# Five engine programs in one critical section: without a block, opened by ScalarE, with semaphores cleared behind waits

## The chip, the cores and the metric

The kernel runs on one core of a Trainium2 chip. The metric is the device time of one execution in microseconds (us); the figure of a version is the median of its runs. The profile shows one execution; its span, from the first to the last recorded instruction, is somewhat shorter than the device time of that same execution.

## The reference

The kernel computes a low-rank (LoRA) update on top of its input. All of it is float32.

```python
batch, seq, d_model, r = 16, 512, 768, 16
# x: (16, 512, 768), A: (768, 16), B: (16, 768), scale = 0.5
def reference(x, A, B, scale):
    lora = np.matmul(np.matmul(x, A), B)
    return (x + scale * lora).astype(np.float32)
```

x has 8192 rows of 768 numbers, 25.2 MB; as much is written. A and B are 48 KB each.

## The kernel before

**Tiles and stages.** The rows are cut into six parts (`PARTS`, 64 tiles of 128 rows in all) that lie in three rooms of SBUF; the first room is used again by the last part. Eight tiles make a group, and there are eight groups. A group passes through five engines: ScalarE casts its first half to 16 bits and GpSimd its second half (`narrowed`, line 167); VectorE transposes both halves in blocks of 32 (`turned`, line 237); TensorE multiplies with A (`projected`, line 270); ScalarE scales the result into a block-diagonal operand (`spread`, line 201); TensorE multiplies with B (`raised`, line 288); VectorE adds the product to x in place (line 250). Ahead of the groups, A and B are loaded and rearranged once (lines 173 to 231, 299 and 206).

**Transfers.** SyncE issues every DMA, all into one queue: the loads of parts 0 and 1 (line 136), A (145), B (149), the loads of parts 2 to 4, and then stores (140) as the sums come, with the two loads of the last part in between as soon as the first room has been stored.

**Order and waits.** The order on every engine is written out by hand, and the engines meet only over semaphores that the kernel counts itself. The programs stand inside `tile_critical`, a section that the framework does not reorder. On entry one engine, SyncE if no other is named, executes a NOP that raises a semaphore (line 129), and all five engines wait for it in a branch (recorded under line 354). Inside the section `nc.Block` gives each engine a block of its own, entered and left by a jump; at the block's end all five engines drain and meet at a barrier (`programs.close()`, line 317). Then GpSimd clears the kernel's semaphores but one in a single range (line 320), waits until the last four stores have landed (line 321) and takes 64 off the remaining one, `s_out` (line 322). On leaving the section, the engine that opened it collects a signal of every engine (under line 129 too), and the framework ends with two barriers of all engines and a clear of its own semaphores (line 354).

Of the kernel before, what the change touches and what calls it, by code (L numbers as in the profile page):

```python
# [26 lines left out]
def kernel(  # L27
# [8 lines left out]
    nc = tc.nc  # L36
# [40 lines left out]
    sems = []  # L77
# [31 lines left out]
    s_ready, s_zero, s_bm = sem("s_ready"), sem("s_zero"), sem("s_bm")  # L109
    s_nact, s_npool = sem("s_nact"), sem("s_npool")  # L110
    s_turned, s_y, s_spread = sem("s_turned"), sem("s_y"), sem("s_spread")
    s_lora, s_sum = sem("s_lora"), sem("s_sum")

    s_free = [sem(f"s_free{p}") for p in range(PAIRS)]
    s_out0, s_out1, s_out = sem("s_out0"), sem("s_out1"), sem("s_out")

    MMS = 2 * NC
    THIRD = MMS // 3
# [7 lines left out]
    STORED = list(dict.fromkeys(groups_for(*st) for st in STORES))  # L126

    section = ExitStack()
    section.enter_context(tc.tile_critical(no_gpsimd_drain=True))  # L129
    programs = ExitStack()  # L130
    block = programs.enter_context(nc.Block(no_gpsimd_drain=True))

    @block.sync
    def _(e):
        def load(ld):
            e.dma_start(out=held(*ld), in_=memory(x2, *ld)).then_inc(s_load[ld], 16)  # L136

        def store(st, done):
            e.wait_ge(s_sum, STORED.index(groups_for(*st)) + 1)
            e.dma_start(out=memory(out2, *st), in_=held(*st)).then_inc(done, 16)  # L140

        load(LOADS[0])
        load(LOADS[1])
        e.wait_ge(s_ready, 1)
        e.dma_start(  # L145
            out=a_rows[0 : NC * APART : APART, :], in_=A.rearrange("(c e) r -> c (e r)", e=64)
        ).then_inc(s_a, 16)
        e.wait_ge(s_brows, 1)
        e.dma_start(out=b_rows[0 : R * APART : APART, :], in_=B).then_inc(s_b, 16)  # L149
        for ld in LOADS[2:5]:  # L150
            load(ld)
        for st, done in zip(STORES, (s_out0, s_out0, s_out1)):
            store(st, done)
        e.wait_ge(s_out0, 32)
        load(LOADS[5])
        e.wait_ge(s_out1, 16)
        load(LOADS[6])
        for st in STORES[3:]:
            store(st, s_out)
# [8 lines left out]
            out=xh[g % 2][:, ds(q * SUB, SUB), :], in_=held(*where[t], SUB)  # L168
        ).then_inc(done, 1)

    @block.gpsimd
    def _(e):
        e.memset(a_rows[0 : NC * APART], 0.0).then_inc(s_ready, 1)  # L173
        e.memset(b_rows, 0.0).then_inc(s_brows, 1)  # L174

        e.sem_inc(s_spread, 1)
        for s in s_free[2:]:
            e.sem_inc(s, 1)
        e.memset(pick, 0.0).then_inc(s_pick, 1)
        e.memset(w_bd.rearrange("p c k m -> p (c k m)").bitcast(fp32), 0.0)  # L180
        for t in y_bd:
            e.memset(t.rearrange("p s m -> p (s m)").bitcast(fp32), 0.0)  # L182
        e.wait_ge(s_pick, 1)
        e.affine_select(  # L184
            out=pick, in_=pick, compare_op=mybir.AluOpType.not_equal, fill=1.0, base=0,
            pattern=[[0, NQ], [-APART, Q]], channel_multiplier=1,
        ).then_inc(s_zero, 1)
        for g in range(NG):
            narrowed(e, e.tensor_copy, s_npool, g, 1)

    @block.scalar
    def _(e):
        e.wait_ge(s_zero, 1)
        e.wait_ge(s_b, 16)
        e.copy(out=b_half, in_=b_rows).then_inc(s_bh, 1)  # L195

        def spread(g):
            e.wait_ge(s_y, g + 1)
            for b in range(NQ):
                q = ds(b * Q, Q)  # L200
                last = e.mul(out=y_bd[g % 2][q, :, q], in_=y_ps[g % 2][q, :, :], mul=sc)  # L201
            last.then_inc(s_spread, 1)

        narrowed(e, e.copy, s_nact, 0, 0)
        e.wait_ge(s_bp, 1)
        e.copy(out=b_mm, in_=lora[0][:, 0, :]).then_inc(s_bm, 1)  # L206
        narrowed(e, e.copy, s_nact, 1, 0)
        for g in range(NG):
            spread(g)
            if g + 2 < NG:  # L210
                narrowed(e, e.copy, s_nact, g + 2, 0)

    @block.vector
    def _(e):
        e.wait_ge(s_a, 16)
        e.transpose(  # L216
            out=a_t[0 : NC * APART].rearrange("i k r c -> i (k r) c"),
            in_=a_rows[0 : NC * APART].rearrange("c (i k r) -> c (k r) i", k=2, r=R),
        ).then_inc(s_ready, 1)
        e.wait_ge(s_ready, 2)  # L220
        EACH = Q // APART
        for b in range(NC // EACH):
            last = e.tensor_copy(  # L223
                out=w_one[:, ds(b * EACH, EACH), :, :],
                in_=a_t[ds(b * Q, Q)].rearrange("i k r (c n) -> i c k r n", n=APART)[..., 0],
            )
        last.then_inc(s_ready, 1)
        e.wait_ge(s_ready, 3)
        e.wait_ge(s_zero, 1)
        for b in range(NQ):  # L230
            e.tensor_copy(out=w_bd[ds(b * Q, Q), :, :, ds(b * Q, R)], in_=w_one)  # L231

        def turned(g):
            for q, s in ((0, s_nact), (1, s_npool)):
                e.wait_ge(s, g + 1)
                v = xh[g % 2][:, ds(q * SUB, SUB), :].bitcast(fp32)
                last = e.transpose(out=v, in_=v)  # L237
            last.then_inc(s_turned, 1)

        turned(0)  # L240
        for p in range(PAIRS):
            e.wait_ge(s_lora, p + 1)
            e.sem_inc(s_free[p], 1)
        for g in range(NG):
            if g + 1 < NG:
                turned(g + 1)
            for p in range(PAIRS):
                xs = held(*where[g * GROUP + 2 * p], 2)
                e.wait_ge(s_lora, (g + 1) * PAIRS + p + 1)
                ins = e.tensor_tensor(  # L250
                    out=xs, in0=xs, in1=lora[p % 2], op=mybir.AluOpType.add
                )
                if g + 1 < NG or p + 2 < PAIRS:
                    ins.then_inc(s_free[p], 1)
                elif p + 1 == PAIRS:
                    ins.then_inc(s_sum, 1)
            if g + 1 in STORED[:-1]:
                e.drain().then_inc(s_sum, 1)  # L258

    @block.tensor  # L260
    def _(e):


        def projected(h, steps):
            if steps[0] == 0:
                e.wait_ge(s_turned, 1)
            xv = xh[h].rearrange("p s (c j k) -> p s c j k", c=NC, k=2)
            for m in steps:
                c, k = divmod(m, 2)
                last = e.matmul(  # L270
                    y_ps[h], w_bd[:, c, k, :], xv[:, :, c, :, k],
                    start=(m == 0), stop=(m == MMS - 1),
                )
            if steps[0] == 0:
                last.then_inc(s_turned, -1)
            elif steps[-1] == MMS - 1:
                last.then_inc(s_y, 1)

        def raised(h, p):
            if p == 0:  # L280
                e.wait_ge(s_spread, 1)
            free = s_free[(p + 2) % PAIRS]
            e.wait_ge(free, 1)
            t = lora[p % 2]
            mms = []
            for k in range(2):
                for n0, w in ((0, 512), (512, 256)) if k == 0 else ((0, 256), (256, 512)):
                    mms.append(e.matmul(  # L288
                        t[:, k, ds(n0, w)], y_bd[h][:, 2 * p + k, :], b_mm[:, ds(n0, w)],
                        start=True, stop=True,  # L290
                    ))
            if p == 0:
                mms[0].then_inc(s_spread, -1)
            mms[1].then_inc(free, -1)
            mms[-1].then_inc(s_lora, 1)

        e.wait_ge(s_bh, 1)
        for n0, w in ((0, 512), (512, 256)):
            last = e.matmul(  # L299
                lora[0][:, 0, ds(n0, w)], pick.rearrange("p b r -> p (b r)"),  # L300
                b_half[:, ds(n0, w)], start=True, stop=True,
            )
        last.then_inc(s_bp, 1)
        e.wait_ge(s_bm, 1)
        with e.Fori(0, NG // 2):
            for h in range(2):
                raised(1 - h, 0)
                raised(1 - h, 1)
                projected(h, range(0, THIRD))
                raised(1 - h, 2)  # L310
                projected(h, range(THIRD, 2 * THIRD))
                raised(1 - h, 3)
                projected(h, range(2 * THIRD, MMS))
        for p in range(PAIRS):
            raised(1, p)

    programs.close()  # L317
    nums = [s.num for s in sems]
    assert nums == list(range(nums[0], nums[0] + len(nums))) and sems[-1] is s_out
    nc.gpsimd.sem_clear(range(nums[0], nums[-1]))  # L320
    nc.gpsimd.wait_ge(s_out, 4 * 16)
    nc.gpsimd.sem_inc(s_out, -4 * 16)
    section.close()


# [33 lines left out]
```

## Time and profile before

| what | value |
|---|---|
| median of 3 runs | 124.8 us (124.76 to 125.47) |
| the profiled execution: its own time | 124.78 us |
| the profiled execution: its span | 122.8 us, 920 instructions |
| VectorE busy | 85.4 us (70%) |
| TensorE matmul busy | 58.1 us (47%) |
| ScalarE, GpSimd busy | 36.8 us, 26.4 us |
| DMA queue of the kernel | 2072 packets, 50.43 MB, 96.7% of 16 engines' span |
| HBM | 25.26 MB read, 25.17 MB written, 411 GB/s over the span |
| mean granted TensorE clock | 0.873 |

How to read it: busy time of an engine counts its datapath alone; branches, semaphore operations and the issuing of DMAs are recorded with a start and a duration but are not busy time. Some 2 us of the execution's time lie outside the span. Engine names with a q (SPq, POOLq) stand for the engine's instruction sequencer, DVE is VectorE, ACT ScalarE, POOL GpSimd, SP SyncE.

### The profile page before, as it was taken

Reading aid. Unit: us, or ns where it says so; the run is one execution under the profiler, and the core shown is the slowest. Engines: PE = TensorE matmul, PEld = TensorE weight load, DVE = VectorE, ACT = ScalarE, POOL = GpSimd, SP = SyncE. Lnnn points to the kernel's source line nnn. Section 1 sums busy time; section 2 is a strip of 40 time slices with the busy share of each in tenths; the row PEclk is TensorE's granted clock in tenths of the full one; section 3 lists DMA queues with packets and bytes.
Section 4 is the critical chain, followed back from the end, with each engine's and each line's share of the span. In section 5 each row is a group of like instructions: output and inputs, shape, how many; then the busy total and the mean of one; then the engine's idle time right before and its main releaser. Section 6 shows DMA issues by size and latency. Waiting matters only on the chain.

```text
span 122.8 us, 920 instructions
## 1 busy us (share of the span) xinstructions
PE 58.1 (47%) x338; PEld 33.5 (27%) x338; DVE 85.4 (70%) x56; ACT 36.8 (30%) x43; POOL 26.4 (22%) x19
## 2 busy tenths in 40 slices
PE   0000239948907944694584389449439645000000
PEld 0000015625503632362252145235224322000000
DVE  0004984089969999989999998999999859600000
ACT  0002958040199141707604080840400310000000
POOL 7703508000196001707100080440000000000000
PEclk9999999999995999769999958999995999655555
DMA  3999999799799895999999999899799799899990
GB/s 104 434 444 402 424 528 464 304 512 480 304 496 496 384 400 222 466 448 400 480 400 448 440 392 528 384 480 464 336 496 451 336 496 464 344 432 408 472 424 32
DMA packets 2073, 50.44 MB, mean 411 GB/s; under 512 B 252, under 2 KB 252, under 8 KB 536
## 3 DMA queue, kind: packets, MB, share of 16 engines
q1 hardware_dynamic: 2072, 50.43, 96.7%
q14 instruction: 1, 0.01, 0.0%
HBM read 25.26 MB, written 25.17 MB: 411 GB/s over the span
## 4 chain that ended last, share of the span: by engine, by line
DVE 40%; DMA 24%; PE 10%; DVEq 5%; ACT 2%; issue 2%; SPq 2%; POOL 1%; POOLq 0%
DMA x_sb<-in_x_dram 24%; DVE x_sb L250 23%; DVE xh L237 17%; PE lora_ps L288 6%; PE ps_yt L270 4%; DVEq L258 4%; ACT xh L167 2%; DVEq L317 1%; POOL a_rows L173 1%; SPq L145 1%; SPq L136 1%; SPq L149 0%; POOLq L354 0%; SPq L129 0%
## 5 line engine op out<-in xcount | busy, mean ns | idle before, releaser
L250 DVE TENSOR_TENSOR x_sb<-x_sb,lora_ps 128x1536 f32<-128x1536 f32 x32 | 54.0, 1738 | 2.6 <-PE lora_ps L288 2.6
L288 PE MATMUL lora_ps<-b_mm,y_bd 128*128 128x512 f16 (+1 forms) x144 | 33.0, 369 | 23.5 <-ACT y_bd L201 9.2
L167 POOL CAST xh<-x_sb 128x3072 f16<-128x3072 f32 x8 | 21.9, 2746 | 54.0 <-DMA x_sb<-in_x_dram 49.3
L270 PE MATMUL ps_yt<-xh,w_bd 128*128 128x256 f16 x192 | 28.9, 297 | 8.6 <-DVE xh L237 8.6
L237 DVE STREAM_TRANSPOSE xh<-xh 128x1536 f32<-128x1536 f32 x16 | 27.5, 1756 | 7.1 <-PE lora_ps L288 5.2
L167 ACT CAST xh<-x_sb 128x3072 f16<-128x3072 f32 x8 | 22.0, 2751 | 14.1 <-DMA x_sb<-in_x_dram 14.0
L270 PEld LDWEIGHTS ps_yt<-xh,w_bd 128*128 128x128 f16 x192 | 19.8, 106 | 18.0 <-DVE xh L237 10.9
L288 PEld LDWEIGHTS lora_ps<-b_mm,y_bd 128*128 128x128 f16 x144 | 13.5, 105 | 38.3 <-issue 24.1
L201 ACT ACTIVATE y_bd<-ps_yt 32x256 f16<-32x256 f32 x32 | 12.0, 374 | 36.1 <-PE ps_yt L270 35.8
L216 DVE STREAM_TRANSPOSE a_t<-a_rows 96x1024 f32<-96x1024 f32 x1 | 1.9, 1926 | 11.0 <-DMA a_rows<-in_A_dram 11.0
L299 PE MATMUL lora_ps<-b_half,pick 128*128 128x512 f16 (+1 forms) x2 | 0.8, 515 | 13.7 <-ACT b_half L195 13.7
L195 ACT ACT_TABLE_LOAD x1 | 1.3, 1283 | 11.6 <-DMA b_rows<-in_B_dram 11.6
L299 PEld LDWEIGHTS lora_ps<-b_half,pick 128*128 128x128 f16 x2 | 0.1, 112 | 13.7 <-ACT b_half L195 13.7
L223 DVE CAST w_one<-a_t 32x128 f16<-32x128 f32 x3 | 1.7, 573 | 0.1
L180 POOL MEMSET w_bd<- 128x1536 f32 x1 | 1.4, 1378 | 0.0
L173 POOL MEMSET a_rows<- 96x1024 f32 x1 | 0.9, 947 | 0.5 <-SPq L129 0.5
L231 DVE COPY w_bd<-w_one 32x384 f16<-32x384 f16 x4 | 1.0, 250 | 0.1
L182 POOL MEMSET y_bd<- 128x512 f32 x2 | 1.0, 521 | 0.0
L195 ACT CAST b_half<-b_rows 128x768 f16<-128x768 f32 x1 | 0.8, 831 | 0.0
L206 ACT CAST b_mm<-lora_ps 128x768 f16<-128x768 f32 x1 | 0.8, 798 | 0.0
L174 POOL MEMSET b_rows<- 128x768 f32 x1 | 0.7, 735 | 0.0
L184 POOL TENSOR_SCALAR_AFFINE_SELECT pick<-pick 128x128 f16<-128x128 f16 x1 | 0.3, 306 | 0.0
(5 smaller groups left out, 0.6 us busy)
## 6 DMA issues: line engine op xcount, KB each, us to landing
x_sb<-in_x_dram SPq DMA_DIRECT2D x2, 6144.0 KB, 36.5
out_dram<-x_sb SPq DMA_DIRECT2D x2, 6144.0 KB, 23.0
x_sb<-in_x_dram SPq DMA_DIRECT2D x3, 3072.0 KB, 15.1
out_dram<-x_sb SPq DMA_DIRECT2D x3, 3072.0 KB, 16.6
x_sb<-in_x_dram SPq DMA_DIRECT2D x1, 2304.0 KB, 9.9
out_dram<-x_sb SPq DMA_DIRECT2D x1, 2304.0 KB, 20.4
x_sb<-in_x_dram SPq DMA_DIRECT2D x1, 768.0 KB, 4.5
out_dram<-x_sb SPq DMA_DIRECT2D x1, 768.0 KB, 15.4
```

Source lines behind the costliest of these rows:

```text
L167: copy(out=xh[g % 2][:, ds(q * SUB, SUB), :], in_=held(*where[t], SUB)).then_inc(done, 1)
L173: e.memset(a_rows[0 : NC * APART], 0.0).then_inc(s_ready, 1)
L180: e.memset(w_bd.rearrange("p c k m -> p (c k m)").bitcast(fp32), 0.0)
L195: e.copy(out=b_half, in_=b_rows).then_inc(s_bh, 1)
L201: last = e.mul(out=y_bd[g % 2][q, :, q], in_=y_ps[g % 2][q, :, :], mul=sc)
L216: e.transpose(out=a_t[0 : NC * APART].rearrange("i k r c -> i (k r) c"), in_=a_rows[0 : NC * APART].rearrange("c (i k r) -> c (k r) i", k= ...
L223: last = e.tensor_copy(out=w_one[:, ds(b * EACH, EACH), :, :], in_=a_t[ds(b * Q, Q)].rearrange("i k r (c n) -> i c k r n", n=APART)[..., 0],)
L237: last = e.transpose(out=v, in_=v)
L250: ins = e.tensor_tensor(out=xs, in0=xs, in1=lora[p % 2], op=mybir.AluOpType.add)
L258: e.drain().then_inc(s_sum, 1)
L270: last = e.matmul(y_ps[h], w_bd[:, c, k, :], xv[:, :, c, :, k], start=(m == 0), stop=(m == MMS - 1),)
L288: mms.append(e.matmul(t[:, k, ds(n0, w)], y_bd[h][:, 2 * p + k, :], b_mm[:, ds(n0, w)], start=True, stop=True,))
```

## The change

The block is gone: the five programs become ordinary functions that are called one after the other inside the section, so that no engine jumps into or out of a block of its own and no barrier stands behind the programs. The section is opened (and its end collected) by ScalarE in place of SyncE. `s_sum` is allocated next to `s_out`, as the last but one. GpSimd now waits for the last of the six counts of `s_sum`, clears the 28 semaphores ahead of it, waits for the last stores, and clears `s_sum` and `s_out` with a second range clear in place of the subtraction.

```diff
-    s_lora, s_sum = sem("s_lora"), sem("s_sum")
+    s_lora = sem("s_lora")
 
     s_free = [sem(f"s_free{p}") for p in range(PAIRS)]
-    s_out0, s_out1, s_out = sem("s_out0"), sem("s_out1"), sem("s_out")
+    s_out0, s_out1 = sem("s_out0"), sem("s_out1")
+
+    s_sum, s_out = sem("s_sum"), sem("s_out")
...
     section = ExitStack()
-    section.enter_context(tc.tile_critical(no_gpsimd_drain=True))
-    programs = ExitStack()
-    block = programs.enter_context(nc.Block(no_gpsimd_drain=True))
-
-    @block.sync
-    def _(e):
+    section.enter_context(
+        tc.tile_critical(sync_engine=mybir.EngineType.Activation, no_gpsimd_drain=True)
+    )
+
+    def on_sync(e):
...
-    @block.gpsimd
-    def _(e):
+    def on_gpsimd(e):
...
-    @block.scalar
-    def _(e):
+    def on_scalar(e):
...
-    @block.vector
-    def _(e):
+    def on_vector(e):
...
-    @block.tensor
-    def _(e):
+    def on_tensor(e):
...
-    programs.close()
+    on_sync(nc.sync)
+    on_gpsimd(nc.gpsimd)
+    on_scalar(nc.scalar)
+    on_vector(nc.vector)
+    on_tensor(nc.tensor)
+
     nums = [s.num for s in sems]
-    assert nums == list(range(nums[0], nums[0] + len(nums))) and sems[-1] is s_out
-    nc.gpsimd.sem_clear(range(nums[0], nums[-1]))
+    assert nums == list(range(nums[0], nums[0] + len(nums))) and sems[-2:] == [s_sum, s_out]
+
+    nc.gpsimd.wait_ge(s_sum, len(STORED))
+    nc.gpsimd.sem_clear(range(nums[0], s_sum.num))
     nc.gpsimd.wait_ge(s_out, 4 * 16)
-    nc.gpsimd.sem_inc(s_out, -4 * 16)
+    nc.gpsimd.sem_clear(range(s_sum.num, s_out.num + 1))
     section.close()
```

## The prediction

> **What bounds the kernel now.** The page gives VectorE 70% and the DMA queue 96.7%, so I first asked for busy times by stretch, with the mean busy share of the 16 DMA engines and the bytes per second in the last two columns:
>
> ```profile
> core 0: us, PE busy (x) PEld busy (x) DVE busy (x) ACT busy (x) POOL busy (x), PEclk, DMA share, GB/s
> 0.00:1.90 1.90, 0.00 (x0) 0.00 (x0) 0.00 (x0) 0.00 (x0) 1.15 (x6) 1.00 0.00 0
> 1.90:3.00 1.10, 0.00 (x0) 0.00 (x0) 0.00 (x0) 0.00 (x0) 1.10 (x3) 1.00 0.89 274
> 3.00:20.00 17.00, 3.44 (x11) 1.30 (x12) 8.09 (x10) 6.87 (x5) 6.30 (x6) 1.00 1.07 448
> 20.00:60.00 40.00, 26.84 (x161) 16.19 (x159) 33.49 (x20) 18.18 (x21) 12.40 (x5) 0.91 0.98 413
> 60.00:100.00 40.00, 25.99 (x160) 15.38 (x160) 37.53 (x24) 11.75 (x19) 5.49 (x2) 0.91 1.01 434
> 100.00:120.00 20.00, 1.83 (x9) 0.62 (x8) 6.31 (x4) 0.00 (x0) 0.00 (x0) 0.63 0.99 428
> 121.60:122.80 1.20, 0.00 (x0) 0.00 (x0) 0.00 (x0) 0.00 (x0) 0.00 (x0) 0.50 0.00 0
> ```
>
> From 3 to 120 us all 16 DMA engines are occupied in every stretch (0.98 to 1.09; packets counted at a stretch's edge push a share over 1). Packet by packet, 16.0 are in flight in every microsecond of that time. The first packet of x starts at 1.98 us and the last ends at 121.57. So the span is three terms: 1.98 us until the first packet, 119.6 us of transfers at full occupancy, and 1.25 us after them. The compute engines and the block's end barrier at 107 us lie beneath the transfers. The change moves no byte, so it can act on the first and third term alone, and only by as much as SyncE's first issue moves, or the steps behind the last landing.
>
> Next the chain of waits, its first pieces (start, duration, what):
>
> ```profile
> 0.67 0.05 issue
> 0.72 0.02 SPq L129
> 0.74 0.02 issue
> 0.77 0.03 POOLq L354
> 0.80 0.15 issue
> 0.95 0.96 POOL a_rows L173
> ```
>
> SyncE's NOP at 0.72 opens the section, and GpSimd passes its branch at 0.77, 41 to 44 ns later. What matters more is SyncE itself, whose first transfers stand in the timeline of its sequencer:
>
> ```profile
> 0.97 0.86 SPq L136 DMA_DIRECT2D x_sb<-in_x_dram  x2
> ```
>
> Last, the steps under lines 354, 320 and 322 (count, shortest/median/longest ns, first and last start):
>
> ```profile
> L354 SPq DRAIN  x3: 7/7/7, 122.1 to 122.4; - x3
> L354 ACTq COMPARE_BRANCH  x1: 33/33/33, 0.8 to 0.8; - x1
> L354 SPq COMPARE_BRANCH  x1: 38/38/38, 0.8 to 0.8; - x1
> L354 PEldq COMPARE_BRANCH  x1: 174/174/174, 0.8 to 0.8; - x1
> L354 POOLq EVENT_SEMAPHORE_RANGE_CLEAR  x1: 67/67/67, 122.5 to 122.5; - x1
> L320 POOLq EVENT_SEMAPHORE_RANGE_CLEAR  x1: 200/200/200, 107.1 to 107.1; - x1
> L322 POOLq EVENT_SEMAPHORE  x1: 17/17/17, 121.9 to 121.9; - x1
> ```
>
> Each engine has exactly one branch at the start, the one that waits. SyncE has three drains at the end, the other engines two. A range clear of 29 semaphores took 200 ns, one of 6 took 67.
>
> **The start, part by part.** The trace's rows, to the nanosecond: the first barrier releases SyncE at 0.655 and ScalarE at 0.659. SyncE's NOP starts at 0.722. The other engines' branches start at 0.763 to 0.777 (TensorE 0.817), SyncE's own only at 0.804: an engine that waits for its own signal passes it 82 ns after giving it, one that waits for another's 41 ns after. The first issue starts at 0.966.
>
> *ScalarE opens.* Its NOP comes at 0.659 + 0.067 = 0.726 (the step from barrier to NOP that SyncE showed); SyncE passes at 0.726 + 0.041 = 0.767 in place of 0.804. That is **-0.037 us** on the path. ScalarE is delayed by about 40 ns instead, which is hidden: its next work waits for B until 11.50. Were SyncE's branch to take TensorE's 174 ns instead of 38, the start would lose 0.10; were the opening to cost nothing, with the issue one ordinary step (0.067) behind the barrier, it would gain 0.966 - 0.722 = 0.24. I take -0.04, which the rows of the other engines show directly.
>
> *No blocks behind jumps.* The plain jumps of the block have no row: between the barrier's end at 107.105 and SyncE's next step at 107.154 a block boundary was crossed in 49 ns, no more than between two steps inside a block (46 ns at 107.33). From SyncE's branch end (0.842) to the issue it is 124 ns, 64 over the 60 ns between the first two issues, and GpSimd shows a similar surplus. That surplus can belong to the waiting branch, which stays, or to a jump that the trace hides. So: 0 to -0.064; I take **0**, since all boundaries that are not waited at cost nothing. [...]
>
> Everything SyncE issues next (second load, A behind GpSimd's memset, B, three loads) follows into the same queue. The first two loads are 3.07 MB, 7 us of transfers at 440 GB/s, so a later issue of A or B by GpSimd's memset costs nothing at the end.
>
> *The block's end.* Drains and barrier from 106.7 to 107.1 vanish, as does the exit's collecting on SyncE at 107.2 to 107.4. The last store runs until 121.57: this is worth 0. If that cover were gone it would be worth 0.4. The added wait for `s_sum` on GpSimd has nothing behind it but the clear: GpSimd's last cast is over by 82 us, and the last sum comes at 106.31. Clearing 28 semaphores then takes some 0.2 us and ends 15 us before the last landing: 0.
>
> **The end, part by part.** Rows: the last of 64 landings counts at 121.910, GpSimd's wait and subtraction 121.934, its NOP 122.030, SyncE's NOP 122.069, SyncE's drains 122.121 and 122.185, the barrier gathered at 122.217, last row 122.796.
>
> *Clear in place of the subtraction.* From the two clears, 133 ns for 23 more semaphores is 5.8 each; two take 67 - 4 x 5.8 = 44 ns against 17, **+0.03**. If the wait can't ride on the clear and becomes a step of its own, another 0.08 (GpSimd's steps follow each other at 78 ns: 122.217 to 122.295). If the following step overlaps (28 ns between the clear at 122.470 and the drain behind it, against 79 behind the subtraction), 0.02 is won. So -0.02 to +0.11.
>
> *ScalarE collects the end.* SyncE's additional drain (64 ns) is now done early, if it is SyncE's whoever opens; ScalarE has only its barrier drain, some 69 ns behind its NOP as at 107.208 to 107.277. The barrier is gathered 122.069 + 0.013 + 0.069 + 0.032 = 122.18 in place of 122.217: **-0.03**, between 0 and -0.064.
>
> **Sum.** -0.04 + 0 + 0.03 - 0.03 = -0.04 us, against the profiled execution's own 124.78 (span 122.83 and 1.95 around it): 124.74. That execution stands 0.02 below the median of the runs, so the forecast is **124.7**. With all terms at their ends: -0.24 - 0.06 - 0.02 - 0.06 = -0.38, and +0.10 + 0.11 = +0.21.
>
> **The rivals.**
>
> *No effect at all.* The waiting branch keeps its 162 ns and what the opening gains is lost in the second clear. Time 124.8. For it: no jump rows; against it: the 41 ns by which SyncE waits for itself are plain.
>
> *The transfers end differently.* Twelve DMA engines finish by 120.66 and four between 121.10 and 121.56, each with packets of 0.91 us. An issue moved by 40 ns can deal the last packets otherwise: evenly, the end comes 0.9 earlier (123.9), with one more packet behind the slowest, 0.9 later (125.7). The three runs differ by 0.71 us already. Against it: nothing in the change alters sizes, order or queue.
>
> *Slower: the table load in front of the opening.* The program of ScalarE, which now opens the section, begins with a load of its activation table:
>
> ```profile
> L195 ACT ACT_TABLE_LOAD  x1: 1283/1283/1283, 11.6 to 11.6; - x1
> ```
>
> Now it stands behind the wait for B, where nobody minds it. With no block boundary between, it could come to stand ahead of ScalarE's NOP; then every engine, SyncE's first issue included, opens later by 1.28 us, and the time is 124.78 + 1.28 = 126.1. It decides from the moment the load precedes the NOP; placed between the NOP and the first cast it costs nothing. Against it: the load is recorded right ahead of the cast that needs it, and the NOP still lies outside the programs.
>
> *Faster by more than 1%.* Were there an instruction fetch behind each jump, removing jumps would take it away. The page counts one packet of the instruction queue in the span (8 KB, 0.31 us, at 93.2 us, while transfers run), none near the start. Even 0.31 and the best of every term give 124.1; passing 1% takes the lucky end of the transfers as well, 123.2. [...]
>
> **How the numbers follow.** A difference of about 1%, 1.25 us, is what a measurement of this kernel tells from no change. Chances: forecast 0.57, no effect 0.18, another end of the transfers 0.11, table load 0.07, the faster case 0.07. The first three lie within 1%: 0.86; slower 0.07, faster 0.07. The range reaches from the terms' ends, 124.4 to 125.0, a step toward the other ends of the transfers on both sides, since the runs before reach 125.47: 124.2 to 125.3.
>
> **What would show it.** After: NOP on ScalarE near 0.73, SyncE's branch near 0.77 and its first issue near 0.93; first packet near 1.95; 119.6 us of transfers; one drain fewer of SyncE behind the last landing; no rows of barrier at 107 us; a clear of some 44 ns at 121.9. Wrong would be: a first issue that moves by more than 0.25 us, transfers shorter or longer by over 1 us, or a step behind the last landing that took over 0.2.

## The result: the span got a little shorter, the time did not

Median after: **125.79 us** (14 runs, 124.67 to 126.33) against 124.72 us before (14 runs beside them, 124.40 to 125.47). The ratio of this set is 1.0067 with a 95% interval of 1.0046 to 1.0088 (the two medians alone stand 0.9% apart). That is less than the 1% that the prediction counts as no change, but the interval excludes no change, and the median lies above the predicted range of 124.2 to 125.3. The profiled execution after took 125.52 us.

The rows of instructions do not show the loss. The first view is the busy times by stretch of the kernel after (columns as in the prediction):

```profile
core 0: us, PE busy (x) PEld busy (x) DVE busy (x) ACT busy (x) POOL busy (x), PEclk, DMA share, GB/s
0.00:1.90 1.90, 0.00 (x0) 0.00 (x0) 0.00 (x0) 0.00 (x0) 1.14 (x6) 1.00 0.00 0
1.90:3.00 1.10, 0.00 (x0) 0.00 (x0) 0.00 (x0) 0.00 (x0) 1.10 (x4) 1.00 0.95 246
...
100.00:120.00 20.00, 2.31 (x13) 0.82 (x10) 6.75 (x4) 0.00 (x0) 0.00 (x0) 0.65 0.99 428
121.60:122.50 0.90, 0.00 (x0) 0.00 (x0) 0.00 (x0) 0.00 (x0) 0.00 (x0) 0.50 0.00 0
```

The transfers fill the span from 1.97 us to 121.18 us as they did before, and the span ends at 122.53 us, 0.30 us *earlier* than in the execution profiled before. The start is seen in the first pieces of the chain of waits (start, duration, what), then in SyncE's first issue in the timeline:

```profile
0.75 0.02 issue
0.78 0.03 POOLq L358
0.81 0.15 issue
0.96 0.96 POOL a_rows L173
```

```profile
0.93 0.85 SPq L137 DMA_DIRECT2D x_sb<-in_x_dram  x2
```

The steps under the lines of the section's exit (count, shortest/median/longest ns, first and last start), with the second clear on line 326:

```profile
L358 SPq DRAIN  x3: 7/7/7, 121.8 to 122.1; - x3
...
L358 SPq COMPARE_BRANCH  x1: 37/37/37, 0.8 to 0.8; - x1
```

```profile
L326 POOLq EVENT_SEMAPHORE_RANGE_CLEAR  x1: 45/45/45, 121.7 to 121.7; - x1
```

SyncE's first issue starts at 0.931 us instead of 0.966, and the new clear takes 45 ns: both as forecast.

Where the time went is seen by subtraction. Every run has its own time and its own span, and I call the difference the **time outside** (spans are given to 0.1 us). In 145 runs of the kernel before (those beside all the experiments below) it is 2.06 us in the mean and never above 2.51. In the 14 runs of the kernel after it is 2.98 us in the mean, while the mean span is 122.65 us against 122.78 before. In the profiled executions it is 125.52 - 122.53 = 3.0 us against 1.95.

The instruction rows end with the span, but packets of the DMA queues are recorded beyond it. First a stretch behind the span of the kernel after, then one of the kernel before (columns as above):

```profile
124.60:125.80 1.20, 0.00 (x0) 0.00 (x0) 0.00 (x0) 0.00 (x0) 0.00 (x0) 0.52 0.07 20
```

```profile
124.00:125.10 1.10, 0.00 (x0) 0.00 (x0) 0.00 (x0) 0.00 (x0) 0.00 (x0) 0.54 0.06 15
```

What moves there is instructions, by the kind that the profile gives their queue. In the kernel after a packet of 8 KB starts at 124.72 us and one of 16 KB at 124.83, which ends at 125.76; in the kernel before one of 16 KB runs from 124.03 to 125.02. The first memset starts 0.24 us into the span in both, and 125.76 - 0.24 = 125.52 and 125.02 - 0.24 = 124.78 are the times of the two executions. So in both the measured time ends with the 16 KB packet, which ends 3.23 us behind the span in place of 2.19.

The values after fall into two clusters. Over all 37 runs of the kernel after (the 14 above and two later sets) 19 lie between 1.8 and 2.43 us, like before, and 18 between 2.88 and 3.63 us, with nothing in between. I call a run **late** if its time outside is 2.8 us or more. Two runs in the table, one of e5 (126.63 us, and the 3.63 above) and one of e13 (127.09), are slow as a whole, over 1.5% above the fastest of their version, and are left out of the ratios alone: without them 17 of 36 runs of the kernel after are late, and e13's mean span is 122.76 us. So the question of the experiments is not what became slower in the span, but what makes some executions end about a microsecond later behind it.

### The profile page after: what moved, and what is told of

It is laid out like the page before. It is cut to its first block, busy times and chain, and to the rows that moved or that the text cites. A ratio compares the mean times of both kernels' runs of the same rounds, so it can differ in the third digit from the quotient of the medians.

```text
span 122.5 us, 908 instructions
## 1 busy us (share of the span) xinstructions
PE 56.9 (46%) x338; PEld 33.2 (27%) x338; DVE 85.7 (70%) x56; ACT 36.8 (30%) x43; POOL 26.5 (22%) x19
## 4 chain that ended last, share of the span: by engine, by line
DVE 40%; DMA 24%; PE 11%; DVEq 5%; ACT 2%; issue 2%; SPq 2%; POOL 1%; POOLq 0%; ACTq 0%
DMA x_sb<-in_x_dram 24%; DVE x_sb L248 23%; DVE xh L235 17%; PE lora_ps L285 6%; PE ps_yt L267 5%; DVEq L256 4%; ACT xh L168 2%; DVEq L131 1%; POOL a_rows L173 1%; SPq L146 1%; SPq L137 0%; SPq L150 0%; POOLq L358 0%; ACTq L131 0%
## 5 line engine op out<-in xcount | busy, mean ns | idle before, releaser
L285 PE MATMUL lora_ps<-b_mm,y_bd 128*128 128x512 f16 (+1 forms) x144 | 32.4, 364 | 25.2 <-ACT y_bd L200 10.6
L267 PE MATMUL ps_yt<-xh,w_bd 128*128 128x256 f16 x192 | 28.3, 293 | 8.4 <-DVE xh L235 8.4
L194 ACT ACT_TABLE_LOAD x1 | 1.3, 1283 | 11.6 <-DMA b_rows<-in_B_dram 11.6
```

The costliest lines, as they stand in the source:

```text
L267: last = e.matmul(y_ps[h], w_bd[:, c, k, :], xv[:, :, c, :, k], start=(m == 0), stop=(m == MMS - 1),)
L285: mms.append(e.matmul(t[:, k, ds(n0, w)], y_bd[h][:, 2 * p + k, :], b_mm[:, ds(n0, w)], start=True, stop=True,))
```

## Experiments

The theories in the order in which they came: (1) the opening by ScalarE does it; (2) the engines have to fetch their closing code from memory, and the changed instruction counts put that fetch at a bad moment; (3) the second range clear does it; (4) the block's end, which the prediction had priced at nothing, evens out the close. The profile records packets of a queue of the kind "instruction": in the kernel after one of 8 KB at 93.04 us of the span (and one of 40 bytes at its start), one of 8 KB at 124.72 and one of 16 KB at 124.83, both behind it. So theory 2 would leave marks that can be moved. Some expectations count as late what lies a little above 2.5 us; the counts here all use 2.8. At the head of a diff, "before" and "after" name the kernel that was edited.

| version | runs | median us | ratio to before (95%) | time outside, mean (range) | late | mean span |
|---|---|---|---|---|---|---|
| before, beside all of these | 145 | | | 2.06 (to 2.51) | 0 | 122.78 |
| after, first set | 14 | 125.79 | 1.0067 (1.0046 to 1.0088) | 2.98 (1.9 to 3.5) | 10 | 122.65 |
| e5, after, second set | 11 | 124.91 | 1.0017 (0.9991 to 1.0043) | 2.54 (1.9 to 3.6) | 4 | 122.65 |
| e18, after, third set | 12 | 125.22 | 1.0018 (0.9992 to 1.0045) | 2.46 (1.8 to 3.5) | 4 | 122.67 |
| e1, after, SyncE opens | 10 | 124.59 | 0.9995 (0.9969 to 1.0021) | 2.11 (1.8 to 3.2) | 1 | 122.64 |
| e2, before, ScalarE opens | 10 | 124.87 | 1.0008 (0.9989 to 1.0026) | 2.25 (1.8 to 2.5) | 0 | 122.68 |
| e3, after, 70 steps on ScalarE | 10 | 124.93 | 1.0017 (0.9990 to 1.0045) | 2.25 (1.8 to 3.4) | 1 | 122.75 |
| e4, after, 70 steps on SyncE | 4 | 125.74 | 1.0125 (1.0053 to 1.0198) | 2.32 (1.8 to 3.2) | 1 | 123.80 |
| e6, after, 8 steps on ScalarE | 11 | 124.83 | 1.0008 (0.9981 to 1.0036) | 2.17 (1.8 to 3.4) | 2 | 122.77 |
| e7, e1 and 5 steps on ScalarE | 11 | 124.83 | 1.0018 (0.9991 to 1.0046) | 2.36 (1.8 to 3.4) | 3 | 122.73 |
| e8, before, 2 steps on ScalarE | 11 | 124.65 | 0.9996 (0.9976 to 1.0015) | 1.98 (1.8 to 2.3) | 0 | 122.80 |
| e9, after, 3 steps on each engine | 12 | 124.90 | 1.0019 (0.9994 to 1.0045) | 2.41 (1.9 to 3.3) | 3 | 122.55 |
| e10, after, 9 steps on each engine | 7 | 125.50 | 1.0060 (1.0035 to 1.0084) | 2.34 (1.8 to 3.0) | 2 | 123.27 |
| e11, after, subtractions at the end | 12 | 125.21 | 1.0039 (1.0011 to 1.0067) | 2.62 (1.8 to 3.5) | 6 | 122.61 |
| e12, after, in the block | 12 | 124.55 | 0.9982 (0.9967 to 0.9997) | 1.93 (1.8 to 2.1) | 0 | 122.63 |
| e17, e12 again | 12 | 124.77 | 0.9993 (0.9974 to 1.0012) | 2.08 (1.7 to 2.4) | 0 | 122.66 |
| e13, after, barrier behind the programs | 12 | 125.21 | 1.0029 (1.0011 to 1.0047) | 2.43 (2.1 to 3.0) | 1 | 122.91 |
| e14, after, barrier ahead of the programs | 12 | 125.32 | 1.0050 (1.0022 to 1.0078) | 2.55 (2.0 to 3.4) | 5 | 122.98 |
| e15, after, ScalarE and TensorE held | 12 | 125.00 | 1.0019 (0.9999 to 1.0040) | 2.35 (2.0 to 2.9) | 1 | 122.69 |
| e16, after, the block's closing steps | 12 | 124.93 | 0.9999 (0.9982 to 1.0016) | 2.12 (1.8 to 2.5) | 0 | 122.80 |

e1 to e4 shared one chip and one set of runs of the kernel before, and so did e5 to e8, e9 to e12, e13 to e15, and e16 to e18.

### Which part: the opening or the block (e1, e2)

e1 takes the opening by ScalarE out of the change; e2 does that part alone.

```diff
 after
-    section.enter_context(
-        tc.tile_critical(sync_engine=mybir.EngineType.Activation, no_gpsimd_drain=True)
-    )
+    section.enter_context(tc.tile_critical(no_gpsimd_drain=True))
```

> The changed kernel with SyncE opening the section as before, the rest of the change kept. Theory A (the microsecond lies behind the span, because an engine's program with another number of instructions has its closing code at another place, where a further 8 KB of instructions has to be fetched behind the last instruction): ScalarE's program gets 2 recorded instructions shorter than in the changed kernel and SyncE's 3 longer, so if one of these two is the engine, the time outside the span falls from 3.0 to 2.0 us and the time to 124.7; if it is GpSimd, VectorE or TensorE it stays at 3 us and 125.7. Rival B (an engine other than SyncE that opens and collects the section makes the program's end slower): 2.0 us outside and 124.7 in any case. Rival C (the second clear is at fault): stays at 125.7. First issue of SyncE again at 0.966 us in all.

```diff
 before
-    section.enter_context(tc.tile_critical(no_gpsimd_drain=True))
+    section.enter_context(
+        tc.tile_critical(sync_engine=mybir.EngineType.Activation, no_gpsimd_drain=True)
+    )
```

> The kernel before with ScalarE opening the section and nothing else changed (blocks, barrier and subtraction kept). Rival B: 125.7, with some 3 us outside the span. Rival C: 124.7. Theory A: ScalarE's program gets longer and SyncE's shorter by a few instructions; 124.7 if the place that matters is not passed, 125.7 if it is, with the extra 8 KB packet behind the span. First issue of SyncE near 0.93 us in all.

Neither moves the median by a measurable amount. But e2 has no late run in 10, and e1, in which SyncE opens again, still has one at 3.23 us. So the opening isn't needed for a late run. It may not be without effect: five of e2's ten runs have 2.43 to 2.53 us outside, more than any of the 25 runs of the kernel before beside them (1.90 to 2.40).

### Moving the instruction fetch (e3, e4)

```diff
 after
+    s_pad = sem("s_pad")
     s_sum, s_out = sem("s_sum"), sem("s_out")
...
     def on_scalar(e):
+        for _ in range(70):
+            e.sem_inc(s_pad, 1)
         e.wait_ge(s_zero, 1)
```

> The changed kernel with 70 semaphore increments at the head of ScalarE's program, where it waits for B until 11.5 us anyway, so they cost nothing in the span (5.5 us at 78 ns each, over by 6.5 us). Theory A with ScalarE as the engine: its code passes the place long before the end, the fetch moves under the transfers, the time outside the span falls to 2.0 us and the time to 124.7. Theory A with another engine, and B and C: stays near 125.7.

In e4 the same 70 steps stand on SyncE, behind its first loads:

```diff
 after
             load(ld)
+        for _ in range(70):
+            e.sem_inc(s_pad, 1)
         for st, done in zip(STORES, (s_out0, s_out0, s_out1)):
```

> The changed kernel with 70 semaphore increments in SyncE's program behind the first loads, where it waits for the first sum from 5 to 35 us, so they cost nothing in the span. Theory A with SyncE as the engine: time outside the span falls to 2.0 us and the time to 124.7. Theory A with another engine, and B and C: stays near 125.7.

In e3 the fetch moved as meant: a packet of 8 KB that lay 2.2 us behind the span's end in the kernel after lies at 9.8 us in e3. One run of 10 is late all the same. e4 brought something else: its span is 1.1 us longer. Its queues, in the view of the DMA:

```profile
q1 hardware_dynamic: 2072, 50.43, 96.0%
q14 instruction: 3, 0.02, 0.0%
```

and the end of its transfers, from the busy times by stretch:

```profile
121.00:122.00 1.00, 0.00 (x0) 0.00 (x0) 0.00 (x0) 0.00 (x0) 0.00 (x0) 0.50 0.06 25
122.00:122.90 0.90, 0.00 (x0) 0.00 (x0) 0.00 (x0) 0.00 (x0) 0.00 (x0) 0.50 0.00 0
```

A further packet of 8 KB now starts at 13.0 us, amid the loads. From 121 to 122 us a share of 0.06 is left, one engine of 16: that one works until 122.43 us, the next-last until 121.54. In the kernel after, the last ends at 121.18. That the packet at 13.0 us holds up this engine is argued from the order of events; no run tested it. The packet itself took 0.32 us, which does not cover 1.1, and the packet at 9.8 us in e3, amid the loads too, had no such effect.

The large instruction packets within these spans are of 8 KB; those of 16 KB lie behind them, in the kernel after at 124.83 us. In e4 something that came with the 70 steps was not hidden beneath the transfers: its mean span is 123.80 us against 122.65.

### The change again, and instruction counts (e5 to e10)

e5 is the kernel after, unaltered.

> The changed kernel itself once more, on the chip of its neighbours here. Theory A (ScalarE's program, through its number of instructions, has its closing code at a place where a fetch of 8 KB is waited for behind the span) expects 125.7 us again, about 3 us outside the span in two of three executions. If it comes out at 124.8, the microsecond hung on the chip and not on the program.

e6 is e3 with 8 steps instead of 70:

```diff
 after
     def on_scalar(e):
+        for _ in range(8):
+            e.sem_inc(s_pad, 1)
```

> The changed kernel with 8 semaphore increments at the head of ScalarE's program, hidden under its wait for B. Theory A: 8 instructions move the place at which the fetch falls due 8 instructions closer to the kernel's end; the time outside the span changes from 3.0 us to between 2.0 and 2.6, the time to 124.8 to 125.2. Rival D (what counts is that ScalarE opens and collects while the blocks are gone, the number of instructions is immaterial): 125.7 and 3 us outside.

e7 adds 5 steps to e1, so that ScalarE executes 58 instructions, as in the kernel after (e1 has 53, three fewer than its expectation reckoned); e8 adds 2 to the kernel before, for the same number.

```diff
 e1
     def on_scalar(e):
+        for _ in range(5):
+            e.sem_inc(s_pad, 1)
```

> The changed kernel with SyncE opening the section, and with 5 semaphore increments in ScalarE's program, so that ScalarE's program has the same number of instructions (58 recorded) as in the changed kernel. Theory A with the number on ScalarE alone deciding: 125.7 us, 3 us outside the span. Rival D, or theory A with SyncE's number deciding: 124.6 as with SyncE opening alone.

```diff
 before
     @block.scalar
     def _(e):
+        for _ in range(2):
+            e.sem_inc(s_pad, 1)
```

> The kernel before with 2 semaphore increments in ScalarE's program, which make it 58 recorded instructions, as many as in the changed kernel; everything else is the kernel before. Theory A with ScalarE's executed instructions deciding: 125.7 us, 3 us outside. If the block's borders take room in the program without being executed, the place isn't met and it stays at 124.8, as rival D expects as well.

e9 and e10 pad all five engines at once. With 3 (GpSimd 2), each executes as many instructions as with the block; 9 go well past that.

```diff
 after
+        for _ in range(3):
+            e.sem_inc(s_pad, 1)
```

(on SyncE behind the first loads, on ScalarE and VectorE at the head of their programs, on TensorE ahead of its wait for `s_bh`; on GpSimd 2 behind its second memset)

> The changed kernel with as many executed instructions on each engine as the kernel with blocks that ScalarE opens: 3 semaphore increments more on SyncE, ScalarE, VectorE and TensorE, 2 on GpSimd, all in idle time. Theory E (the time outside the span scatters up to 3.6 us in some executions because the closing code of SyncE, GpSimd, VectorE or TensorE lies at another place in the instruction stream; executed instructions count): back to 1.8 to 2.5 us outside in every execution, median 124.8. Rival F (the barrier at the block's end, not the number of instructions, keeps the closing together): executions of 2.9 us and more outside stay, two or more of them in ten. Rival C (the second clear): they stay as well.

```diff
 after
+        for _ in range(9):
+            e.sem_inc(s_pad, 1)
```

(in the same places; on GpSimd 8)

> The changed kernel with 9 semaphore increments more on each engine (8 on GpSimd), which match the kernel with blocks if the borders of a block take room in the stream without showing as executed instructions. Theory E with that count: 1.8 to 2.5 us outside in every execution, median 124.8. Rivals F and C: executions of 2.9 us and more outside stay.

The second set of the change has a ratio of 1.0017 where the first had 1.0067, with 4 late runs in 11 where there were 10 in 14. The effect is a share of executions, and that share differs between sets, so the median of one set is a poor measure of it.

For theory 2 in the form that a program's number of instructions decides, these runs are bad. e8 has ScalarE's count of the kernel after and no late run in 11; e7 has the same count and 3 in 11; e9, with the block's counts on every engine and no block, has 3 in 12. The 8 KB packet did follow ScalarE's count where it is recorded (2.2 us behind the span's end at 58 instructions, 0.3 us at 66), but moving it left late runs in e6 and e3. As the cause, the place of this packet is out. That it adds to their number isn't excluded: e3, e6 and e1 together have 4 late in 31, less than the 18 in 37 of the change. The 16 KB packet is another matter: none of these edits was made to move it, and the part on what is open comes back to it.

e10's longer span has a place in its trace: in the closing, ScalarE's first drain starts 361 ns behind its NOP, in the kernel after 57 ns. Why isn't shown.

### The second clear, and the block with everything else (e11, e12)

```diff
 after
-    nc.gpsimd.sem_clear(range(s_sum.num, s_out.num + 1))
+    nc.gpsimd.sem_inc(s_sum, -len(STORED))
+    nc.gpsimd.sem_inc(s_out, -4 * 16)
```

> The changed kernel with two subtractions, of s_sum and s_out, in place of the second clear. Rival C: 1.8 to 2.4 us outside in every execution, 124.7. Theory E and rival F: executions of 2.9 us and more outside stay, some four in ten, median 124.9 to 125.7.

```diff
 after
+    programs = ExitStack()
+    block = programs.enter_context(nc.Block(no_gpsimd_drain=True))
 
-    def on_sync(e):
+    @block.sync
+    def _(e):
...
-    on_sync(nc.sync)
...
+    programs.close()
```

> The changed kernel with the block kept: ScalarE opens, the clears stand behind their waits, only the programs stand in blocks of their own with the barrier behind them. Theory E and rival F: no execution over 2.6 us outside, median 124.8. Rival C: executions of 2.9 us and more, median 125 or more.

This pair divides the change in two. Without the second clear 6 of 12 are late; with it and ScalarE's opening, but inside the block, none of 12, and all twelve lie between 1.8 and 2.1 us. Theory 3 is out, and what is missing in the kernel after is something of the block.

### What of the block: three partial substitutes (e13 to e15)

```diff
 after
     on_tensor(nc.tensor)
+    nc.all_engine_barrier()
```

> The changed kernel with one barrier of all engines behind the five programs and ahead of GpSimd's clears, without a block. Rival F (the barrier at the block's end keeps the closing together): 1.8 to 2.5 us outside the span in every execution, median 124.6 as with the block kept. Rival G (not the barrier, but the places of code that the block's borders make): executions of 2.8 us and more outside stay, a third of them or more, median 124.9 to 125.7.

```diff
 after
+    nc.all_engine_barrier()
     on_sync(nc.sync)
```

> The changed kernel with the same barrier of all engines ahead of the five programs. It delays SyncE's first issue by about 0.4 us, so the span is 123.0. If only the late barrier matters (F): executions of 2.8 us and more outside stay. If the number of instructions or of barriers matters and not their place in time: 1.8 to 2.5 us outside in every execution, as then behind the programs too. Rival G: they stay.

```diff
 after
+    s_late = nc.alloc_semaphore("s_late")
...
                 e.drain().then_inc(s_sum, 1)
+        e.drain().then_inc(s_late, 2)
...
     on_scalar(nc.scalar)
+    nc.scalar.wait_ge(s_late, 1)
+    nc.scalar.sem_inc(s_late, -1)
     on_vector(nc.vector)
     on_tensor(nc.tensor)
+    nc.tensor.wait_ge(s_late, 1)
+    nc.tensor.sem_inc(s_late, -1)
```

> The changed kernel with ScalarE and TensorE held behind their programs until VectorE has made the last sum (one wait each, no barrier), so that no engine is at the section's end ahead of 106 us, as with the block, but without a meeting of all. If it is the early arrival of these two (ScalarE at 97.6, TensorE at 104) that spreads the closing: 1.8 to 2.5 us outside in every execution, 124.6. If it takes the meeting of all engines (F), or code places (G): executions of 2.8 us and more stay.

The reason for e15 is in the steps under line 131 of the kernel after, the section's own collecting of its engines:

```profile
L131 ACTq EVENT_SEMAPHORE  x3: 17/38/38, 97.6 to 107.4; - x3
...
L131 ACTq DRAIN  x1: 1477/1477/1477, 97.7 to 97.7; - x1
L131 PEldq DRAIN  x1: 870/870/870, 103.5 to 103.5; - x1
L131 DVEq DRAIN  x1: 2442/2442/2442, 104.4 to 104.4; - x1
```

Without the block's end, ScalarE is through its program at 97.6 us and TensorE at 104.4; with it, both stay until all have met at 107.1. A barrier ahead of the programs (e14) leaves 5 late in 12 and adds 0.3 us to the first packet (2.31 us against 1.97). Holding engines at the end is another matter: e13 and e15 have 1 late in 12 each, 2 in 24 against 18 in 37. Their other runs aren't quite as before either, with means of 2.38 and 2.30 us against 2.06. Nor is there a gap at 2.8 us in these two: their late runs have 2.98 and 2.91 us, the next 2.66 and 2.58. So holding the engines at the end goes with fewer late runs, not with none, and e13's median of 125.21 us is not the 124.6 that was expected of a barrier that does it all.

### The block's closing steps without the block (e16 to e18)

The deciding set, on one chip: e16 is the kernel after with the drains and the barrier that the block would have executed, written out behind the plain functions; e17 is e12 again, e18 the kernel after again.

```diff
 after
     on_tensor(nc.tensor)
+    for e in (nc.scalar, nc.tensor, nc.vector, nc.sync):
+        e.drain()
+    nc.all_engine_barrier(sem_only=True)
```

> The changed kernel with the very instructions that the block puts behind the programs (a drain of four engines, the barrier of five by semaphores alone), but without a block, so that every engine executes the same instructions in the same order as in the next kernel, which keeps the block. If the end of the block does it (its drains and barrier together with the place that they give to the closing code): 1.8 to 2.4 us outside the span in every execution, and the same time as the next kernel, 124.6. If it is the block's borders alone, marks that are not executed (G): executions of 2.6 us and more stay, a third or more, median 125.0 or more.

> The changed kernel with the block kept, once more: ScalarE opens, both clears stand behind waits, programs in blocks. All theories that blame the block's removal: no execution over 2.5 us outside, 124.55 to 124.7, and no slower than the kernel before. If the earlier run of it owed its 0.9982 to its chip: 124.8 and some executions over 2.5.

> The changed kernel itself a third time, beside the two others on one chip. All theories: 2.8 us and more outside the span in a third to two thirds of the executions, median 124.9 to 125.8, span 122.65. Were it as even as the block's version here, the difference would hang on the chip.

There are four drains because the block drains four engines, not all five: GpSimd's rows under line 317 of the kernel before are semaphore steps alone. In e16 the four have their rows under the line of the loop, and run while the transfers do:

```profile
L320 ACTq DRAIN  x1: 1556/1556/1556, 95.4 to 95.4; - x1
L320 PEldq DRAIN  x1: 870/870/870, 101.4 to 101.4; - x1
L320 DVEq DRAIN  x1: 2440/2440/2440, 102.3 to 102.3; - x1
L320 SPq DRAIN  x1: 131/131/131, 105.1 to 105.1; - x1
```

e16 has 0 late in 12, with 2.12 us outside; e17 0 in 12, with 2.08; e18 4 in 12, with 2.46. With 0 in 24 against 4 in 12 this one set could still be luck (of all ways to place four late runs among these 36, 1 in 120 puts all four on e18), but it does not stand alone. Every version that executes the block's closing steps (e2, e8, e12, e16, e17 and the kernel before) has none: 0 in 57 beside 0 in 145. Every version that lacks them has some. And since e16 has no blocks and no jumps into or out of them, the closing steps suffice without the blocks. That last step rests on twelve runs: 0 in 12 for e16 alone beside 4 in 12 would come by chance once in 21 times. The medians of e16 and e17 both lie above the 124.6 that was expected. A fetch behind each jump, which the faster rival of the prediction supposed, shows no price here: e17 with its jumps has a median of 124.77 us, e16 without them 124.93.

e16 differs from e13 in little: GpSimd is not drained in e16, and the other four engines signal the barrier in a step of their own behind the drain. Which of these takes away the rest of the late runs isn't separated, and 0 in 12 against 1 in 12 is no difference by itself.

**A version that beats both?** The block kept, with ScalarE's opening and the clears (e12, e17), gives ratios of 0.9982 (0.9967 to 0.9997) and 0.9993 (0.9974 to 1.0012): a gain of 0.2% and of 0.1%, and the second interval includes no change. It has none of the late runs of the kernel after, and is hardly different from the one before.

## Why the prediction was right and wrong

**Right: what bounds the span.** Only the first and the third term of the span were to change. The transfers lasted from 1.967 to 121.179 us, 119.2 us against 119.6, with the same packets. The mean spans differ by -0.13 us (122.65 against 122.78).

**Right: ScalarE opens.** SyncE's branch starts at 0.769 us (forecast 0.767, before 0.804) and the first issue at 0.931: -0.035 us against -0.037. The first packet came 0.016 us earlier in this execution (1.967 against 1.983).

**Right: no blocks behind jumps, 0.** From the end of SyncE's branch to the first issue it is 125 ns, 124 before. The surplus that could have been a hidden jump is still there without the jumps, so it isn't theirs.

**Slightly off: clear in place of subtraction.** The clear took 45 ns, 44 forecast. But the next step follows 89 ns behind its start, where it followed 96 ns behind the subtraction: -0.007 us instead of +0.03. The step's duration was right; it had simply been hidden in the interval to the next one.

**Right sum, wrong detail: ScalarE collects the end.** From GpSimd's NOP to the gathered barrier it is 163 ns against 187, so -0.024 us (forecast -0.03). SyncE still shows three drains behind the last landing, not one fewer: its first simply begins earlier. (The prediction's "the other engines two" holds for three of them; GpSimd had three drains at the end as well.) From the last landing to the last row it is 0.89 us against 0.92.

**Right to give it little: the table load in front of the opening.** The load is still recorded at 11.6 us, ahead of its cast, so that rival's 126.1 did not come about. The rival of transfers that end differently named 125.7 for its bad side, near the measured median; but the transfers ended *earlier* (121.18 against 121.57), so the agreement is chance.

**Two slips in the working, neither of weight.** 124.74 with the 0.02 added is 124.76, which rounds to 124.8 and not to 124.7; the range holds both. And the first two loads, 2304 and 768 KB of 1024 bytes, are 3.15 MB, not 3.07, still some 7 us of transfers.

**Wrong: the block's end, and the 1.95 us around the span.** The failed steps are "this is worth 0" for the drains and the barrier at 107 us, and a sum that took "1.95 around it" as a constant of the machine. Inside the span the first was right: nothing on the path waited for the barrier. Behind the span its removal costs 2.68 - 2.06 = +0.62 us in the mean over all 37 runs of the kernel after (+0.92 in the first 14), against -0.12 us in the span. In the profiled execution the term measured 2.99 us in place of 1.95. The prediction also said "if that cover were gone it would be worth 0.4", but the cover never went: the loss is of another kind. Its list of what would show it wrong held events in the span only. None of them occurred, so the rows within the span would have confirmed a forecast that the clock refuted.

**Open: why the instructions come late.** Of 20 executions, one of each version and of both kernels, there is a trace, and behind the span it holds packets and semaphore updates. Five of the 20 are late (the kernel after, e7, e10, e11, e14). Each of the five has a 16 KB packet of instructions that starts 1.81 to 2.31 us behind the span and ends 3.19 to 3.35 us behind it, and its time is, to 0.01 us, the stretch from the first memset to that end. In eight of the other 15 such a packet ends 2.00 to 2.79 us behind the span, in seven there is none. The last semaphore update of the closing comes 2.06 to 2.19 us behind the span in the late five and 1.90 to 2.19 us in the others; in the seven executions in which no instruction packet ends later, the time ends 0.11 us behind that update. So in the traces it is not the engines' closing steps that are late, but a fetch of instructions. Theory 2 had the right kind of event, though its experiments aimed at another packet. Which engine the 16 KB are for, whether they are waited for, and why they come late without the block's closing steps stays open; no run was made to move them.

Shown is when the microsecond comes (not in 202 runs with the block's closing steps, in 18 of 37 of the kernel after, in 26 of 113 of the altered versions without them) and what isn't needed for it: the opening, the second clear, the instruction counts, the place of the 8 KB packet. That it matters how far apart the engines finish their programs (ScalarE at 97.6 us, VectorE at 106.9) is argued from e13 and e15 only.

## What to carry to other kernels

Subtract the span from the time in every run before and after, and look at its spread, not at one value: here 2.06 us of the time lay, in the mean, outside the span before and 2.68 after, and an edit to steps that end at 107.1 us, 15.7 us ahead of the span's end, showed there. Packets are recorded beyond the last row (here until 3.23 us behind it), so see there what the time ends with. The drains and the barrier at the block's end, at 97.1 to 107.1 us beneath transfers that lasted until 121.57, were no gain to remove: the mean span fell by 0.12 us with the whole change, the time outside grew by 0.62. Write them out if the blocks go, as e16 did (2.12 us outside, none late in 12). And where a median moves between sets of the same kernel (1.0067, 1.0017, 1.0018), count how many executions are of which kind before explaining its size.

## What the runs showed of the hardware that was not expected

- The time behind the span has two clusters in the kernel after, 1.8 to 2.43 and 2.88 to 3.63 us, while the spans of both kinds are alike (122.62 us in the mean of the late runs, 122.69 in the others).
- In 13 of 20 executions the measured time ends, to 0.01 us, with a packet of instructions behind the last row (16 KB in 12 of them, 8 KB in e5); in all five late ones it is one of 16 KB, which ends 3.19 to 3.35 us behind the span.
- 70 one-step semaphore instructions on SyncE, all beneath the transfers, made the span 1.1 us longer (e4: 123.8 against 122.65 us), with one more 8 KB instruction packet at 13.0 us; 70 on ScalarE, whose added packet came at 9.8 us, added only 0.1 (122.75).
- In the two profiled executions the engine that opens the section starts its own branch 82 and 83 ns after its NOP; SyncE, ScalarE and GpSimd start theirs 38 to 45 ns after another's NOP, VectorE 49 and 55, TensorE 88 and 95: handing the opening to an engine whose work starts late is a gain of 0.035 us on the path in the trace, too small for the medians to show.
